# Layer 0's seams reordered, and some attention biases in another pool, in a two-layer FNet/Hyena/attention backbone

## The chip, the cores and the metric

The kernel runs on one core of a Trainium2 chip. The core has a matrix engine (TensorE, PE in the profile), VectorE (DVE), ScalarE (ACT) and GpSimd (POOL). SyncE (SP) has no arithmetic here: its queue issues DMA transfers, strictly in order, and so does GpSimd's queue beside its own work. PEld is TensorE's loading of the stationary operand. On-chip memory is SBUF, and matmuls accumulate in PSUM.

The metric is the device time of one execution in microseconds (us). A profiled execution also gives a span, from the first to the last instruction. The granted clock is the share of its full clock at which TensorE was allowed to run in a stretch.

## The reference

The model has two layers over 1024 latent tokens (a 16 x 64 grid, width 1024) with 256 context tokens, in float32. Each layer is a mixer and a SwiGLU feed-forward part (FFN) of hidden width 2816, and each of the two is preceded by an RMS norm and modulated by six vectors (shift, scale and gate, twice) that come from a conditioning vector:

```python
def ada_mod(cond, w, b):
    m = (jax.nn.silu(cond) @ w + b)[..., None, :]
    return jnp.split(m, 6, axis=-1)

def swiglu(u, w_gate, w_up, w_down):
    return (jax.nn.silu(u @ w_gate) * (u @ w_up)) @ w_down

def mixer_ab(u, w_in, w_out, conv_w, conv_b, w1, b1, freq, w2, b2, w3, skip):
    p = u @ w_in
    y_f = fourier_mix(p[..., :FOURIER_CH])
    y_h = hyena_mix(p[..., FOURIER_CH:], conv_w, conv_b, w1, b1, freq, w2, b2, w3, skip)
    return jnp.concatenate([y_f, y_h], axis=-1) @ w_out
```

Latent tokens are conditioned by `c`, context tokens by `c_ctx`. Layer 0's mixer is `mixer_ab`: four groups of channels through a two-dimensional Fourier transform, the others through a Hyena operator with two long convolutions. Layer 1's mixer is neighbourhood attention of 16 heads, in which a latent query sees an 8 x 32 window of the grid, with a relative position bias and a mask of columns, and all context keys. Layer 1 gives no context output. A final RMS norm ends the model.

## The kernel before

Activations stand with the channels on the 128 partitions, as eight blocks, and with the tokens on the free axis, in pieces `pc`: 0 and 1 are the two halves of the latent tokens (512 each), 2 is the context (256). Matrix products are made of three matmuls: every operand is split into a high part (a cast to fp32r, on ScalarE, line 350) and a low part (source less high, on VectorE, line 352), and TensorE sums high x high, high x low and low x high (`lin`, and `mm` in line 346). So a weight goes through four steps: its load by SP into a stage tile `ws` (a pool of four) or a wide tile `s` (pool `S4`), the cast to `wh`, the subtraction to `wl`, and 24 matmuls for one block of 128 outputs. In a block of the context, 256 tokens wide, the first two of every three matmuls use `wh` alone, so TensorE begins when `wh` is there and stands at the third if `wl` is not.

The order on each engine is made by a scheduler from the program's generators. `follow(x)` holds what is issued under it behind instruction `x` in the order; a `yield` in a generator is a place at which other work may be put. A tile of a pool is reused in turn, and the instruction that first writes it waits for the last reader of its previous use. SP works in order: a load that waits for its tile holds all loads behind it.

The four places that matter here follow each other in time.

`out_proj` (from about 640 us) is layer 0's output projection. While it runs, `late_groups` computes a group of modulation vectors on VectorE: `load_cond` loads `c` and `c_ctx`, broadcast to all partitions, in four pieces, and applies SiLU to each on ScalarE (line 556); products and row sums are line 584. Just before it, the last Hyena inverse transform ends with splits of its result `y` (`inverse_last`). An eviction (line 1739) adds a projected block to the residual `h`; `square` (lines 609 and 614) sums its squares over the blocks into a tile `tk`.

The first FFN (from 751 us) begins with the context: for each of 22 blocks `fb`, 24 matmuls of `gate` and 24 of `up`, SiLU of the gate (line 2011) and its product with up (line 2012). `rms_begin` turns the sums of squares into row sums with eight narrow matmuls, a square root and a reciprocal, and `rms_end` broadcasts the result over the partitions. From block 2 on, `wino_second` prepares, block by block, the second half of the latent operands for a Strassen-Winograd product that follows (lines 1809 to 1842).

`down` is the FFN's last product. Its latent part ends near 1494 us; then comes the context part, 22 blocks `kb` of 24 matmuls (line 2230), while `after2` norms the finished latent pieces for layer 1, block by block: two instructions on VectorE (lines 656 and 659) and one on ScalarE (658) for each.

The attention (until about 2080 us) goes through 64 items. An item loads a bias for two column groups of a head; items of the column groups 0 and 1 (`c0 == 0`) take two tiles of pool `G` for it, the others one `ws` tile. Line 2443 takes the maximum of the context scores, 2446 joins local scores and bias and reduces, 2448 and 2450 are the exponentials. In items before the 48th (`cross`) the exponentials of the context are transposed by DMA, from a tile of pool `TK`; in the last sixteen TensorE transposes them. In these last items SP also loads the attention's output back (`load_o`, `s<-d`) for the output projection.

Of the kernel before, what the change touches and what calls it, by code (L numbers as in the profile page):

```python
# [10 lines left out]
F32 = mybir.dt.float32  # L11
F32R = mybir.dt.float32r
F16 = mybir.dt.float16
AF = mybir.ActivationFunctionType
# [244 lines left out]
class Builder:  # L259
# [333 lines left out]

    def late_groups(self, ms, where):

        self.load_cond(wide=where == "s4")
        for m in ms:
            yield from self.ada_group(0, m, (0, 1), where)

# [815 lines left out]
    def inverse_last(self, y, fl):  # L1415

        nc, a = self.nc, self.a
        V = nc.vector
        C, x, late = [], [], []

        def product(acc, first, cb, m, e, i, f):
            yh, yl = (q[:, cb * P:cb * P + P] for q in self.y_of(1, i, f))
            d = acc[cb][:, e * 256:e * 256 + 256]
            for k, (s, w) in enumerate(((yh, m[:, :256]), (yh, m[:, 256:]), (yl, m[:, :256]))):
                nc.tensor.matmul(d, s, w, start=cb not in first, stop=e == 1 and i == 1 and f == 3 and k == 2,
                                 skip_group_check=True)
                first.add(cb)

        next(fl)
        for r in (0, 1):  # L1430
            acc = [self.PS() for _ in range(4)]
            first = set()
            ms = self.cmat2(a["vke_l"][r], True)
            for e, m in enumerate(ms):
                for cb in range(4):
                    for f in (0, 1):
                        product(acc, first, cb, m[:, f * 512:f * 512 + 512], e, 2 * e, 2 * r + f)
            yield
            if r == 0:
                next(fl)  # L1440
            else:
                for _ in fl:
                    yield
            ms = [self.cmat2(a["vko_l"][r, :, c:c + 2048], True) for c in (0, 2048)]
            if r:
                for cb in range(4):
                    x.append(self.S4())
                    self.ld(x[cb], self.xd[1][cb][:, :LAT])
            sa = [self.TK(), self.TK()]
            sa = [t[:, i:i + 256] for t in sa for i in (0, 256)]  # L1450
            for cb in range(4):
                for e, i in ((0, 3), (1, 1)):
                    for h, m in enumerate(ms[e]):
                        for f in (0, 1):
                            product(acc, first, cb, m[:, f * 512:f * 512 + 512], e, i, 2 * h + f)
                    if e == 0:
                        nc.scalar.copy(sa[cb], acc[cb][:, :256])
                A, B = sa[cb], acc[cb][:, 256:]
                t = self.G() if r == 0 else self.T()
                V.tensor_tensor(t[:, :256], A, B, ADD)  # L1460
                rv = t[:, 256:][:, ::-1]
                if r == 0:
                    V.tensor_tensor(rv, A, B, SUB)
                    C.append(t)
                    continue
                V.tensor_tensor(rv, B, A, SUB)
                y.t.update(self.new_act(pcs=(0, 1), wide=False, blocks=(4 + cb,)).t)
                v = self.T()
                V.tensor_tensor(v, C[cb], t, ADD)
                V.tensor_tensor(C[cb], C[cb], t, SUB)  # L1470
                V.tensor_tensor(v, v, x[cb][:, :512], MUL)
                self.split(v, y.ap(0, 4 + cb, 0), y.ap(1, 4 + cb, 0))
            yield
        for cb in range(4):
            V.tensor_tensor(C[cb], C[cb], x[cb][:, 512:], MUL)
            self.split(C[cb], y.ap(0, 4 + cb, 1), y.ap(1, 4 + cb, 1))

    def inverse_c(self, o, y):
        nc, a = self.nc, self.a
# [494 lines left out]
        s.to(2)  # L1974
        return s

    def ffn(self, l, u, h, hs, second, after, keep=None, begun={}):

        nc, a = self.nc, self.a
        n2 = NFB // 2  # L1980
# [19 lines left out]
        if l == 0:  # L2000
            self.pad(self.pt, PAD_T)
        if u is not None:
            for fb in range(NFB):
                wide = 3 if fb < NFB - 2 else 2
                gh, gl = self.weights(a["gate"][l, fb], wide=wide)
                uh, ul = self.weights(a["up"][l, fb], wide=wide)
                lo = self.last_lo
                ga = self.lin(gh, gl, 0, range(KB), u, (2,))[2]
                ua = self.lin(uh, ul, 0, range(KB), u, (2,))[2]
                t = self.T()  # L2010
                nc.scalar.activation(t[:, :256], ga[:, :256], AF.Silu)
                nc.vector.tensor_tensor(t[:, :256], ua[:, :256], t[:, :256], MUL)
                self.ldr(hidc[fb // 2][:, fb % 2], t[:, :256])
                if fb >= 2:
                    with self.follow(last):
                        next(second, None)
                last = lo
            self.load_cond(act=False)
            todo = (x for l1, m in [(0, 5)] + [(1, m) for m in range(6)]
                    for x in self.ada_group(l1, m, (0, 1) if l1 == 0 or m < 2 else (0,), "s4"))  # L2020
# [16 lines left out]
        for i in range(NFB // 2):  # L2037
# [26 lines left out]
            gate = dict(self.res)  # L2064
            for k in ((0, 0), (1, 1), (0, 1)):
                nc.scalar.activation(gate[k], gate[k], AF.Silu)
            t = self.G()
# [345 lines left out]
    def attn_item(self, head, hd, hf, c0, qs, kk, kc, vt, osb, out, cross):  # L2413

        nc, a = self.nc, self.a
# [3 lines left out]
        if c0:  # L2419
            t = self.W("ws", "bias", F32, 768)  # L2420
            self.ld(t.rearrange("p (i k) -> p i k", i=2), a["bias"][head, hf, c0:c0 + 2].rearrange("i p k -> p i k"))
            bias = [t[:, :384], t[:, 384:]]
        else:
            bias = [self.G(F32, 384), self.G(F32, 384)]
            for i in (0, 1):
                self.ld(bias[i], a["bias"][head, hf, c0 + i])
        for i in (0, 1):
            c = c0 + i
# [3 lines left out]
        for i in (0, 1):  # L2432
            c = c0 + i
# [10 lines left out]
        pc = self.T()  # L2444
        for i in (0, 1):
# [3 lines left out]
                                 bias=mn[:, i:i + 1])  # L2449
# [10 lines left out]
        for k, src, n in turns:  # L2460
# [3 lines left out]
            t = self.S2(F16, 1024)  # L2464
# [6 lines left out]
        if not osb:  # L2471
            t = self.S4()
            osb.update({0: t[:, :512], 1: t[:, 512:]})
        for i in (0, 1):
            c = c0 + i
# [14 lines left out]
        for i in (0, 1):  # L2490
            c = c0 + i
# [39 lines left out]
    def run(self):  # L2531
        nc, a = self.nc, self.a
# [9 lines left out]
        def drain(g):  # L2542
            for _ in g:
                pass

        u = Act()
# [90 lines left out]
        h = Act()  # L2637
        u = None

        def load_h(pcs):  # L2640
            for pc in pcs:
                for b, t in enumerate(self.load_x(pc)):
                    h.put(0, b, pc, t)

        uf = Act()
        hs0 = [self.DR([P, 1280]) for _ in range(KB)]
        hs1 = [self.DR([P, 1280]) for _ in range(KB)]

        def spill(h, hs, pcs):
            for pc in pcs:  # L2650
                for b in range(KB):
                    self.ldr(hs[b][:, pc * 512:pc * 512 + WID[pc]], h.ap(0, b, pc))

        rest = []

        def after1(pcs):
            spill(h, hs0, pcs)
            if 2 in pcs:
                uf.t.update(self.new_act(pcs=(2,)).t)
                rs = self.rms(pcs)  # L2660
                for b in range(KB):
                    self.norm_block({b: h.ap(0, b, 2)}, b, 2, 0, 3, uf, rs[0])
                load_h((1,))
                rest.append(rs[1])
            else:
                drain(first)
                rest.append(self.rms((1,))[0])

        def first_row():
            yield from self.wino_first(h, 0, 3, rest.pop())  # L2670

        first = first_row()

        load_h((2, 0))
        self.out_proj("w_out", y, [(2, 0), (1,)], h, 0, 2, after1, first, late)
        for b in range(8):
            self.tap(f"h1_{b}", h.ap(0, b, 0))
        u1 = Act()
        hd = [self.DR([P, LAT]) for _ in range(KB)]

        def after2(pc):
            c = self.rms_begin(pc)
            yield
            r = self.rms_end(pc, c)
            yield
            for b in range(KB):
                if b % 2 == 0:
                    u1.t.update(self.new_act(pcs=(pc,), blocks=(b, b + 1)).t)
                self.norm_block({b: h3.ap(0, b, pc)}, b, pc, 1, 0, u1, r)
                if b % 2:  # L2690
                    yield

        h3 = Act()
        self.ffn(0, uf, h3, hs0, (x for r in rest for x in self.wino_second(h, 0, 3, r)), after2, hd)
        for b in range(8):
            self.tap(f"h2_{b}", h.ap(0, b, 0))
        for i, _ in enumerate(self.values(u1)):
# [62 lines left out]
        for i, _ in enumerate(first_part(1)):  # L2760
            if i == 7:
                c = self.rms_begin(0)
# [53 lines left out]
        begun = {(0, 0): self.wino_begin(1, 0, 0, self.G)}  # L2816
        c = self.rms_begin(1)
# [87 lines left out]
```

## Time and profile before

| | us |
|---|---|
| time, median of 3 runs (2848.43 to 2850.37) | 2848.94 |
| the profiled execution | 2850.4 |
| its span | 2848.5 |
| TensorE busy | 2762.6 (97%) |
| VectorE busy | 2044.6 (72%) |
| ScalarE busy | 1319.0 (46%) |
| GpSimd busy | 543.9 (19%) |

In rows of a timeline the first column is the start from the span's beginning, the second the duration of the group, then engine, line, operation, output and inputs by name, their shape, and the count; brackets hold the idle time of the engine just before and the instruction that ended it. A row of a busy engine says nothing of what the time depends on; an idle time of TensorE does, since it works 97% of the span.

### The profile page before, as it was taken

Reading aid. Unit: us, or ns where it says so; the run is one execution under the profiler, and the core shown is the slowest. Engines: PE = TensorE matmul, PEld = TensorE weight load, DVE = VectorE, ACT = ScalarE, POOL = GpSimd, SP = SyncE. Lnnn points to the kernel's source line nnn. Section 1 sums busy time; section 2 is a strip of 40 time slices with the busy share of each in tenths; the row PEclk is TensorE's granted clock in tenths of the full one; section 3 lists DMA queues with packets and bytes.
Section 4 is the critical chain, followed back from the end, with each engine's and each line's share of the span. In section 5 each row is a group of like instructions: output and inputs, shape, how many; then the busy total and the mean of one; then the engine's idle time right before and its main releaser. Section 6 shows DMA issues by size and latency. Waiting matters only on the chain. (4 is left out here: it accounts for less than half of the span.)

```text
span 2848.5 us, 43624 instructions
## 1 busy us (share of the span) xinstructions
PE 2762.6 (97%) x15610; PEld 2314.2 (81%) x15610; DVE 2044.6 (72%) x3531; ACT 1319.0 (46%) x2269; POOL 543.9 (19%) x880
## 2 busy tenths in 40 slices
PE   7999999999999999999999999999999999999998
PEld 4876778788898888888879888888887788888887
DVE  6767577867877888876777437778768977664556
ACT  5433336443554333333455337788755533333434
POOL 2210235331001221222020002333211122112000
PEclk9999999999999999999999999999999999999999
DMA  7356535665666656658884436877855366434763
GB/s 268 121 182 219 155 93 186 215 211 189 214 196 200 211 196 210 213 202 323 306 305 152 133 115 152 201 197 197 243 191 207 133 239 229 140 106 170 234 195 133
DMA packets 296886, 554.20 MB, mean 195 GB/s; under 512 B 81872, under 2 KB 128658, under 8 KB 296670
## 3 DMA queue, kind: packets, MB, share of 16 engines
q1 hardware_dynamic: 227966, 352.67, 39.4%
q0 software_dynamic: 61504, 185.65, 18.6%
q10 hardware_dynamic: 7200, 13.11, 1.4%
q8 instruction: 123, 2.02, 0.3%
q14 instruction: 93, 0.76, 0.1%
HBM read 405.01 MB, written 118.76 MB: 184 GB/s over the span
## 5 line engine op out<-in xcount | busy, mean ns | idle before, releaser
L1932 PE MATMUL ps<-s,s 128*128 128x512 f32 x2012 | 497.6, 391 | 3.5 <-DVE s L1823 1.9
L1932 PEld LDWEIGHTS ps<-s,s 128*128 128x128 f32 x2012 | 378.3, 188 | 84.0 <-DVE s L1823 3.2
L346 PE MATMUL ps<-s,wh 128*128 128x256 f32 (+1 forms) x1776 | 401.9, 331 | 10.8 <-ACT s L1043 3.2
L346 PEld LDWEIGHTS ps<-s,wh 128*128 128x128 f32 x1776 | 295.2, 190 | 46.4 <-ACT s L350 4.1
L346 PE MATMUL ps<-s,wl 128*128 128x256 f32 (+1 forms) x888 | 267.4, 329 | 1.7 <-DVE wl L352 1.6
L2109 PE MATMUL ps<-s,s 128*128 128x512 f32 (+1 forms) x1000 | 259.9, 383 | 3.3 <-DVE s L352 3.2
L350 ACT CAST s<-s 128x1024 fp32r<-128x1024 f32 (+2 forms) x192 | 172.6, 927 | 193.1 <-DMA s<-d 177.3
L346 PE MATMUL pq<-s,wh 128*128 128x512 f32 (+1 forms) x848 | 260.8, 389 | 0.4 <-ACT wh L350 0.3
L352 DVE TENSOR_TENSOR wl<-ws,wh 128x1024 fp32r<-128x1024 f32 (+1 forms) x141 | 168.3, 1195 | 119.8 <-ACT wh L350 114.2
L350 ACT CAST wh<-ws 128x1024 fp32r<-128x1024 f32 (+1 forms) x141 | 144.7, 1026 | 204.9 <-PE ps L346 85.0
L352 DVE TENSOR_TENSOR s<-s,s 128x1024 fp32r<-128x1024 f32 (+2 forms) x170 | 190.9, 1154 | 59.4 <-ACT s L350 59.1
L346 PE MATMUL ps<-s,s 128*128 128x65 f16 (+4 forms) x2736 | 226.2, 235 | 7.3 <-DVE st L2446 2.6
L350 ACT CAST s<-t 128x512 fp32r<-128x512 f32 (+2 forms) x238 | 133.9, 581 | 195.8 <-PE ps L1932 69.2
L2109 PEld LDWEIGHTS ps<-s,s 128*128 128x128 f32 x1000 | 184.5, 188 | 41.3 <-DVE s L352 5.0
L352 DVE TENSOR_TENSOR s<-t,s 128x512 fp32r<-128x512 f32 (+2 forms) x238 | 151.2, 651 | 72.6 <-ACT s L350 59.6
L1932 PE MATMUL ps<-s,wh 128*128 128x512 f32 x624 | 194.9, 390 | 0.0
L346 PEld LDWEIGHTS ps<-s,wl 128*128 128x128 f32 x888 | 165.6, 190 | 18.4 <-DVE wl L352 2.5
L337 POOL DMA_DIRECT2D d<-s x186 | 101.0, 544 | 375.5 <-DVE s L1739 92.5
L346 PEld LDWEIGHTS pq<-s,wh 128*128 128x128 f32 x848 | 151.1, 190 | 22.1 <-ACT wh L350 0.7
L346 PE MATMUL pq<-s,wl 128*128 128x512 f32 (+1 forms) x424 | 162.0, 382 | 0.6 <-DVE wl L352 0.6
L2109 PE MATMUL ps<-s 128*128 128x512 f32 (+1 forms) x500 | 150.9, 385 | 0.0
L346 PEld LDWEIGHTS ps<-s,s 128*128 128x128 f32 (+1 forms) x816 | 126.6, 192 | 21.8 <-ACT t L2448 2.7
(486 smaller groups left out, 5465.0 us busy)
## 6 DMA issues: line engine op xcount, KB each, us to landing
s<-d SPq DMA_DIRECT2D x282, 256.0 KB, 3.9
d<-s POOLq DMA_DIRECT2D x170, 256.0 KB, 3.7
s<-in_down SPq DMA_DIRECT2D x150, 256.0 KB, 4.2
s<-in_ada_w POOLq DMA_DIRECT2D x64, 512.0 KB, 4.9
ws<-in_up SPq DMA_DIRECT2D x44, 512.0 KB, 3.7
d<-g POOLq DMA_DIRECT2D x86, 256.0 KB, 3.0
ws<-in_gate SPq DMA_DIRECT2D x42, 512.0 KB, 4.8
d<-tk POOLq DMA_DIRECT2D x66, 256.0 KB, 4.0
```

Of the source, the lines that this page charges most:

```text
L337: self.last_ldr = self.nc.gpsimd.dma_start(out, in_).ins
L346: self.last_mm = self.nc.tensor.matmul(o, l, r, start=st, stop=sp).ins
L350: self.last_hi = nc.scalar.copy(hi, src).ins
L352: self.last_lo = eng.tensor_tensor(lo, src, hi.bitcast(F32), SUB).ins
L1932: nc.tensor.matmul(ps, x[:, sl], y, start=first and j == 0 and x is wh and y is xh, stop=j == 3 and x is wl, skip_group_check=True)
L2109: m = nc.tensor.matmul(acc[j][:, c0:c1], x[:, sl], y[:, xs], start=first and k == 0, stop=last and k == 2, skip_group_check=True)
```

## The change

1. `late_groups` loads the conditions without their SiLU, yields three times more, and then applies the four SiLUs behind the last cast of the inverse transform (`inv_hi`).
2. The row-sum matmuls of the second latent half are no longer made at the end of `out_proj` but as the first step of the work that goes along with the FFN's blocks: `rms_begin` behind block 0, `rms_end` behind block 1, and `wino_second` from block 2 on as before. The gate weight of block 0 is loaded and split earlier, during `wino_first`, and `p3 = 1` sets which tiles it takes.
3. `after2` norms the second latent half one block at a time, each behind the low split of a weight.
4. In attention items with `c0 == 0` that are neither `cross` nor of a pair's second head (`hd`), the two biases take tiles of pool `TK` in place of pool `G`.

```diff
     def late_groups(self, ms, where):
 
-        self.load_cond(wide=where == "s4")
+        self.load_cond(wide=where == "s4", act=False)
+        yield
+        yield
+        yield
+        with self.follow(self.inv_hi):
+            for t in self.cond:
+                for x in t:
+                    self.nc.scalar.activation(x, x, AF.Silu)
...
         for cb in range(4):
             V.tensor_tensor(C[cb], C[cb], x[cb][:, 512:], MUL)
             self.split(C[cb], y.ap(0, 4 + cb, 1), y.ap(1, 4 + cb, 1))
+        self.inv_hi = self.last_hi
...
         if u is not None:
+            last = None
             for fb in range(NFB):
                 wide = 3 if fb < NFB - 2 else 2
-                gh, gl = self.weights(a["gate"][l, fb], wide=wide)
+                gh, gl = early.pop() if fb == 0 else self.weights(a["gate"][l, fb], wide=wide)
...
-                if fb >= 2:
-                    with self.follow(last):
-                        next(second, None)
+                with self.follow(last):
+                    next(second, None)
                 last = lo
...
-            bias = [self.G(F32, 384), self.G(F32, 384)]
+            new = self.G if cross or hd else self.TK
+            bias = [new(F32, 384), new(F32, 384)]
...
                 drain(first)
-                rest.append(self.rms((1,))[0])
 
         def first_row():
-            yield from self.wino_first(h, 0, 3, rest.pop())
+            for k, _ in enumerate(self.wino_first(h, 0, 3, rest.pop())):
+                if k == 6:
+                    self.p3 = 1
+                    early.append(self.weights(a["gate"][0, 0], wide=3))
+                yield
...
+            los = []
             for b in range(KB):
                 if b % 2 == 0:
                     u1.t.update(self.new_act(pcs=(pc,), blocks=(b, b + 1)).t)
-                self.norm_block({b: h3.ap(0, b, pc)}, b, pc, 1, 0, u1, r)
-                if b % 2:
+                with self.follow(los.pop() if los and pc == 1 else None):
+                    self.norm_block({b: h3.ap(0, b, pc)}, b, pc, 1, 0, u1, r)
+                los.append(self.last_lo)
+                if b % 2 or pc == 1:
                     yield
...
+        def second():
+            with self.follow(self.last_mm):
+                c = self.rms_begin(1)
+            yield
+            with self.follow(self.last_mm):
+                r = self.rms_end(1, c)
+            yield
+            yield from self.wino_second(h, 0, 3, r)
```

What this does to the order is seen best at three places. In the rows a tile's name ends in a running number, which tells one use of a tile from another; lines after the first edit carry numbers that are some 7 to 9 higher than before.

VectorE at the FFN's blocks 2 and 3, before (`wl_7626` is the low part of gate 3's weight, `t_7547` the product of block 1):

```order
L352 TENSOR_TENSOR wl_7559<-s_2061_7557,wh_7558 128x1024
L1835 SCALAR_TENSOR_TENSOR s_1699_6932<-s_1699_6932,c_97,t_7269 128x512
L1823 TENSOR_TENSOR s_2069_7621<-s_1711_6980,s_2069_7621 128x512
L1842 TENSOR_TENSOR s_1725_7060<-s_1699_6932,s_1725_7060 128x512
L352 TENSOR_TENSOR wl_7626<-s_2070_7624,wh_7625 128x1024
L1823 TENSOR_TENSOR s_2079_7692<-s_1725_7060,s_2079_7692 128x512
L2012 TENSOR_TENSOR t_7547<-ps_7522,t_7547 128x256
```

and now (`t_7613` is the product of block 2, from up 2's result `ps_7588`):

```order
L352 TENSOR_TENSOR wl_7559<-s_2061_7557,wh_7558 128x1024
L2021 TENSOR_TENSOR t_7539<-ps_7514,t_7539 128x256
L1843 SCALAR_TENSOR_TENSOR s_1698_6930<-s_1698_6930,c_97,t_7543 128x512
L1843 SCALAR_TENSOR_TENSOR s_1699_6932<-s_1699_6932,c_97,t_7543 128x512
L1850 TENSOR_TENSOR s_1711_6980<-s_1698_6930,s_1711_6980 128x512
L1850 TENSOR_TENSOR s_1725_7060<-s_1699_6932,s_1725_7060 128x512
L1831 TENSOR_TENSOR s_2069_7621<-s_1711_6980,s_2069_7621 128x512
L1831 TENSOR_TENSOR s_2079_7692<-s_1725_7060,s_2079_7692 128x512
L2021 TENSOR_TENSOR t_7613<-ps_7588,t_7613 128x256
L352 TENSOR_TENSOR wl_7626<-s_2070_7624,wh_7625 128x1024
```

The first steps of `wino_second` and the product of block 2 now stand ahead of gate 3's low split.

VectorE in the context part of `down`, before (`t` and `s` belong to the norm, `wl` to the weights):

```order
L352 TENSOR_TENSOR wl_14519<-ws_14517,wh_14518 128x1024
L656 SCALAR_TENSOR_TENSOR t_14583<-s_3020_12687,c_99,t_14505 128x512
L656 SCALAR_TENSOR_TENSOR t_14587<-s_3021_12689,c_99,t_14505 128x512
L656 SCALAR_TENSOR_TENSOR t_14630<-s_3022_12691,c_99,t_14505 128x512
L656 SCALAR_TENSOR_TENSOR t_14634<-s_3023_12693,c_99,t_14505 128x512
L656 SCALAR_TENSOR_TENSOR t_14674<-s_3078_12968,c_99,t_14505 128x512
L659 SCALAR_TENSOR_TENSOR s_3328_14581<-t_14583,c_99,s_3328_14581 128x512
L352 TENSOR_TENSOR wl_14553<-ws_14551,wh_14552 128x1024
```

and now:

```order
L352 TENSOR_TENSOR wl_14519<-ws_14517,wh_14518 128x1024
L663 SCALAR_TENSOR_TENSOR t_14583<-s_3020_12687,c_99,t_14505 128x512
L666 SCALAR_TENSOR_TENSOR s_3328_14581<-t_14583,c_99,s_3328_14581 128x512
L352 TENSOR_TENSOR wl_14553<-ws_14551,wh_14552 128x1024
L663 SCALAR_TENSOR_TENSOR t_14624<-s_3021_12689,c_99,t_14505 128x512
L352 TENSOR_TENSOR wl_14596<-ws_14594,wh_14595 128x1024
L663 SCALAR_TENSOR_TENSOR t_14664<-s_3022_12691,c_99,t_14505 128x512
L666 SCALAR_TENSOR_TENSOR s_3329_14582<-t_14624,c_99,s_3329_14582 128x512
L666 SCALAR_TENSOR_TENSOR s_3341_14662<-t_14664,c_99,s_3341_14662 128x512
L352 TENSOR_TENSOR wl_14634<-s_3338_14632,wh_14633 128x1024
```

The norm's instructions now stand one to three between two splits.

SP in the last attention items, before (`s<-d` are the loads of the attention's output):

```order
L331 DMA s_4641_22126<-d_15887 128x512
L331 DMA g_22037<-in_bias 128x384
L331 DMA s_4642_22128<-d_15888 128x512
L331 DMA g_22038<-in_bias 128x384
L331 DMA bias_22343<-in_bias 128x2x384
```

and now:

```order
L331 DMA tk_21637<-in_bias 128x384
L331 DMA bias_21736<-in_bias 128x2x384
L331 DMA tk_22037<-in_bias 128x384
L331 DMA t_21520<-d_15137 32x4x128 x4
L331 DMA tk_22038<-in_bias 128x384
L331 DMA bias_21948<-in_bias 128x2x384
L331 DMA bias_22131<-in_bias 128x2x384
L331 DMA s_4584_21804<-d_15877 128x512
```

The two biases of this item moved from the end of the stream of `s<-d` loads to a place ahead of its first one.

More of the change, by code (lines that the diff above doesn't have):

```diff
@@ L1975, in wino_begin, with ffn @@
         return s
-    def ffn(self, l, u, h, hs, second, after, keep=None, begun={}):
+    def ffn(self, l, u, h, hs, second, after, keep=None, begun={}, early=()):
         nc, a = self.nc, self.a
@@ L2652, in spill @@
                     self.ldr(hs[b][:, pc * 512:pc * 512 + WID[pc]], h.ap(0, b, pc))
-        rest = []
+        rest, early = [], []
         def after1(pcs):
@@ L2688, in after2 @@
                     u1.t.update(self.new_act(pcs=(pc,), blocks=(b, b + 1)).t)
-                self.norm_block({b: h3.ap(0, b, pc)}, b, pc, 1, 0, u1, r)
-                if b % 2:
+                with self.follow(los.pop() if los and pc == 1 else None):
+                    self.norm_block({b: h3.ap(0, b, pc)}, b, pc, 1, 0, u1, r)
+                los.append(self.last_lo)
+                if b % 2 or pc == 1:
                     yield
         h3 = Act()
-        self.ffn(0, uf, h3, hs0, (x for r in rest for x in self.wino_second(h, 0, 3, r)), after2, hd)
+        def second():
[6 more added lines that the diff above has]
+            yield from self.wino_second(h, 0, 3, r)
+        self.ffn(0, uf, h3, hs0, second(), after2, hd, early=early)
         for b in range(8):
```

## The prediction, made before the changed kernel was run

> **What bounds the kernel now.** I read the shares of busy time first, then the waits of TensorE from 500 us on, then the narrow stretches around the largest of them.
>
> ```profile
> PE 2762.6 (97%) x15610; PEld 2314.2 (81%) x15610; DVE 2044.6 (72%) x3531; ACT 1319.0 (46%) x2269; POOL 543.9 (19%) x880
> ```
>
> TensorE works 97% of a span of 2848.5 us: 85.9 us are idle in all, and an edit that leaves the matmuls alone can win only what lies in that, or in slow matmuls. So each of the four places of the change is read by one question: does TensorE stand still there, and who ends the standstill? The rows of the waits name a line, the releaser, the sum in us, how often, and the longest:
>
> ```profile
> PE ps L2230 <- DVE wl L352: 3.0, 2, 2.1
> PE ps L346 <- DVE st L2446: 2.6, 1, 2.6
> ...
> PE pq L346 <- DVE tk L614: 2.3, 1, 2.3
> ...
> PE ps L346 <- DVE wl L352: 1.6, 1, 1.6
> ```
>
> These four rows are the four places: `down`'s context part (two waits, 0.91 and 2.10), the attention's last items (2.57), the first FFN's start (2.29), and `out_proj` (1.63). A wait costs more than itself where the granted clock falls behind it. The columns of the next view are: stretch, its length, PE busy, PEld, DVE, ACT, POOL busy, the granted clock, DMA share, GB/s.
>
> ```profile
> 756.20:759.60 3.40, 3.40 (x19) 3.40 (x18) 2.23 (x4) 2.31 (x6) 0.00 (x0) 0.50 0.89 276
> ...
> 1537.90:1541.30 3.40, 3.40 (x16) 3.40 (x17) 3.40 (x5) 0.72 (x1) 0.00 (x0) 0.50 0.57 194
> ...
> 2060.10:2063.50 3.40, 3.40 (x14) 3.01 (x14) 2.15 (x7) 1.53 (x4) 0.30 (x1) 0.50 1.04 318
> ...
> 2070.30:2073.70 3.40, 3.32 (x35) 3.03 (x35) 1.88 (x7) 3.12 (x8) 0.00 (x0) 0.51 0.32 126
> ```
>
> Right behind the waits of 2.29, 2.10 and 2.57 us (and behind a pair of 0.94 and 0.97 at 2058 to 2060) TensorE runs 3.4 us at half clock, which loses 3.4 x 0.5 = 1.7 us each time. Behind the 1.63 in `out_proj` it does not:
>
> ```profile
> 670.80:674.20 3.40, 3.17 (x19) 2.83 (x20) 3.40 (x10) 0.00 (x0) 0.54 (x1) 1.00 0.60 184
> ```
>
> So I count a wait of about 2 us or more as itself plus 1.7, a shorter one as itself. The Trainium skill, "TensorE: Matmul & The Clock Gate", section "HAM oscillation — how this bites in real kernels", sets the limit higher: no idle gap of TensorE over about 3.4 us. The half clock in these rows follows standstills of 2.1 to 2.6 us, so the rows decide; what the time would be if the rule held is a rival below.
>
> **A: SiLUs of the conditions, `out_proj` (1.63 and a small 0.17 us).** The rows below are ScalarE's, then VectorE's.
>
> ```profile
> 654.18 0.63 ACT L556 ACTIVATE s<-s 128x512 f32<-128x512 f32 x1 [0.71 <-DMA s<-in_c_ctx]
> 654.72 1.64 ACT L350 CAST s<-g 128x512 fp32r<-128x512 f32 x3
> ```
> ```profile
> 653.50 0.69 DVE L352 TENSOR_TENSOR s<-t,s 128x512 fp32r<-128x512 f32 x1 [3.98 <-ACT s L350]
> ...
> 669.76 1.22 DVE L352 TENSOR_TENSOR wl<-ws,wh 128x1024 fp32r<-128x1024 f32 x1
> ```
>
> Four SiLUs wait one by one for the broadcast loads of c and c_ctx; casts of y's last splits stand behind them in ScalarE's order, and VectorE idles 3.98 us for them. It then works without a pause until the weight split at 669.76, which TensorE waits for. With the casts ahead of the SiLUs, five of those splits (one of 0.69, four more of the same form) fall into that idle time, so some 2 to 3 us leave the backlog, which is more than the 1.63 wait. The SiLUs themselves are bound by their loads (the last lands at about 654.2), and ScalarE's casts before them need no DMA, so the adaLN products are not later. Gain 1.63 + 0.17 = **1.8**; bounds 0 (the backlog stays, since adaLN products change places too) and 1.8.
>
> **B: the first FFN's start (2.29 us, then half clock).**
>
> ```profile
> 751.33 0.39 PE L346 MATMUL ps<-s,wl 128*128 128x512 f32 x1
> 754.01 1.05 PE L346 MATMUL pq<-c,tk 128*128 128x1 f32 x8 [2.29 <-DVE tk L614]
> ```
> ```profile
> 754.19 2.36 DVE L352 TENSOR_TENSOR wl<-s,wh 128x1024 fp32r<-128x1024 f32 x2 [0.24 <-ACT wh L350]
> ...
> 769.54 0.42 DVE L2012 TENSOR_TENSOR t<-ps,t 128x256 f32<-128x256 f32 x1
> 769.99 1.23 DVE L352 TENSOR_TENSOR wl<-s,wh 128x1024 fp32r<-128x1024 f32 x1
> ```
> ```profile
> 776.00:781.44 5.44, 5.44 (x50) 5.44 (x49) 4.75 (x7) 2.89 (x4) 0.54 (x1) 1.00 0.53 170
> ```
>
> The eight row-sum matmuls wait for the last eviction's square. The change puts them behind the second projection (up) of block 0 and has gate 0's weight split some 10 us earlier, so gate 0 starts at once: 2.29 + 1.7 = 3.99 go. Two waits come in. First, up 0's low half is split after the same eviction, as the first of the two at 754.19, and ends near 755.4. A projection of 24 matmuls takes 5.44 / 2 = 2.72 us (the row of 776.00 is one block), so gate 0 would end at 751.72 + 2.72 = 754.44, and up 0's third matmul, 0.22 later, waits 0.7. Second, the order of VectorE now has the gate-times-up product of block 2 *ahead of* the low split of gate 3, where before it stood behind it. That product needs up 2's last matmul, so gate 3's third matmul comes only a product and a split after that: 0.42 + 1.23 less the 0.22 of its first two matmuls, 1.4 us. Behind it gate 4's split stands ahead of the product again. Gain 3.99 - 0.7 - 1.4 = **1.9**. Bounds: 3.3 if gate 3 doesn't stall, 0.2 if that stall grows towards 2 us and brings a half clock (-1.7). Two more table loads on ScalarE fall in blocks where it works 2.89 of 5.44 us (row above); without that cover they would cost what they last.
>
> **C: `down`'s context part (0.91 and 2.10 us, then half clock).**
>
> ```profile
> 1527.45 3.40 DVE L656 SCALAR_TENSOR_TENSOR t<-s,c,t 128x512 f32<-128x512 f32 x5
> ...
> 1531.42 1.22 DVE L352 TENSOR_TENSOR wl<-ws,wh 128x1024 fp32r<-128x1024 f32 x1
> ...
> 1536.54 1.22 DVE L352 TENSOR_TENSOR wl<-ws,wh 128x1024 fp32r<-128x1024 f32 x1
> ```
> ```profile
> s<-in_down SPq DMA_DIRECT2D x150, 256.0 KB, 4.2
> ```
>
> Five norm instructions (3.40 us) run in one piece ahead of a split that TensorE needs at 1531.8, and seven more ahead of the next. After the change one to three stand between two splits. A block of weights lasts 24 matmuls, 2.72 us; a split and two norm instructions of 3.40 / 5 = 0.68 are 1.22 + 1.36 = 2.58, so VectorE just keeps pace. Removed: 3.01 + 1.7 = 4.71. What comes in is on the queue of SP: the wide tile that holds every fifth weight now gets its load behind that of a narrow one, which waits until a split has freed a tile.
>
> ```profile
> 1532.67 5.48 SPq L331 DMA_DIRECT2D ws<-in_down  x2
> ```
>
> Before, such a load went out at 1532.67, right after the split that began at 1531.42; with only two norm instructions ahead of that split it comes about 1 us earlier, and the wide load with it, near 1531.7. With 4.2 us to land (the row is of 256 KB; I take it for these of 512 KB too), the cast of 1.0 and the split of 1.22 that weight is ready near 1538.1, against a need at 1536.9: 1.2 us, and by the same walk 0.3 at the next of them. Gain 4.71 - 1.5 = **3.2**; bounds 4.7 (loads in time) and 0.5 (the first of them misses by 2.2, with a half clock).
>
> **D: biases of four of the last sixteen items (2.57 us, then half clock).**
>
> ```profile
> 2059.35 0.33 SPq L331 DMA_DIRECT2D g<-in_bias  x1
> ```
> ```profile
> 2069.70 0.62 DVE L2446 CUSTOM_DVE_ANT_0 g<-ps,g,st 128x384 f32<-128x384 f32 x1 [3.21 <-DMA g<-in_bias]
> ```
>
> The bias of such an item waits for a G tile, is issued at 2059.35 in the middle of the stream that loads the attention's output, and lands 10 us later behind it; the reduce holds the score's PSUM, and TensorE stops. In the other pool its load stands ahead of that stream. That pool has four tiles and, in these items, no other user, since the transposes of the first part are done; I find none of its four loads waiting for a tile, and what stands behind them (loads of t, the stream) comes earlier, not later. Gain 2.57 + 1.7 = **4.3**. Above it: ScalarE's wait at 2054.31
>
> ```profile
> 2054.31 0.84 ACT L350 CAST wh<-ws 128x768 fp32r<-128x768 f32 x1 [1.61 <-DMA ws<-in_w_out]
> ```
>
> is behind the pair of 0.94 and 0.97 with its half clock. If the stream, some 3.5 us earlier, makes room for that load, 0.94 + 0.97 + 1.7 = 3.6 go as well: upper bound 7.9. I take none of it, since the DMA engines stay full (share 1.04 in the row of 2060.10). Lower bound 0, a rival below.
>
> **Sum.** 1.8 + 1.9 + 3.2 + 4.3 = 11.2. The profiled execution took 2850.4, 1.9 outside its span, and is the slowest of three; from the median 2848.9 the sum gives **2838**. Its own range: all losses, 0 + 0.2 + 0.5 + 4.3 = 5.0, gives 2844; all gains, 1.8 + 3.3 + 4.7 + 7.9 = 17.7, gives 2831.
>
> **The rivals.**
>
> *Each seam gets its stall back* (0.17). B's gate 3 and C's first wide tile both stall 2 us or more, with a half clock each: 1.8 + 0.2 + 0.5 + 4.3 = 6.8, **2842**. For it: the half clock needs only about 0.5 us more than I give these two waits. Also, untouched waits of 1.6 to 1.8 us elsewhere may come to lie otherwise and get one, 1.7 each: 2844. Against it: the walks give 1.4 and 1.2.
>
> *All goes, the pair at 2058 too* (0.15): **2831**, as above.
>
> *The half clock doesn't come from these waits* (0.06). Then it stays, somewhere, and only bare waits go: 1.80 + 2.29 + 3.01 + 2.57 - 0.7 - 1.4 - 1.5 = 6.1, **2843**. Against it: each of the rows with 0.50 starts at or soon after the end of such a wait. The rule of the Trainium skill named above would make it so.
>
> *D doesn't do what it says* (0.06): a load of the new tiles waits for its tile on SP and holds the stream. Gain 1.8 + 1.9 + 3.2 = 6.9, **2842**.
>
> *Slower* (0.06): VectorE becomes the bound of the FFN's first part. It works 4.75 of 5.44 us in a block already. If the product stayed ahead of the next gate's low split in all following blocks, each would cost the 1.4 us of gate 3; against the gains of the rest, 1.8 + 3.2 + 4.3 + 3.99 - 0.7 = 12.6, nine blocks break even, and nineteen cost 26.6: 2849 + 14 = **2863**. Against it: the order has the split ahead again at gate 4, and 0.69 us a block are free to catch up.
>
> **How the numbers follow.** Forecast 0.50, rivals as given. What can be told from no change is 0.2% or 5.7 us, so faster means below 2843.2: nearly all of the forecast (0.48), all of the second rival (0.15), and a good half of those at 2842 to 2843 (0.14) make 0.77; slower 0.06; within it 0.17. The range 2830 to 2846 takes in all cases but the slower one and half clocks at several untouched waits.
>
> **What would show it.** Right: no wait of TensorE on wl in `out_proj`; gate 0 directly behind `out_proj`'s last matmul, a wait of 0.7 at up 0 and of 1.4 at gate 3; full clock at about 754 to 758, 1534 to 1540 and 2062 to 2072; norm instructions singly between splits; the biases landed before 2040. Wrong: a new wait of 2 us or more at gate 3 or at a wide tile, SP standing before a bias of the new pool, or half clocks that remain where no wait precedes them.

## The result, and the profile after

| | us |
|---|---|
| changed kernel, median of 11 runs (2837.0 to 2849.5) | 2843.3 |
| before, 11 runs (2848.4 to 2861.4) | 2850.4 |
| ratio, 95% interval | 0.997 (0.9957 to 0.9983) |
| the changed kernel a second time, 6 runs against 11 of before, ratio | 0.9966 (0.9953 to 0.9978) |
| profiled executions: before, after | 2850.4, 2839.6 |

The change makes the kernel 0.30% to 0.34% faster, 8.6 to 9.7 us of 2850; the first interval allows 4.8 to 12.3 us. The forecast was 11.2 us less, 2838, with a range of 2830 to 2846. The two profiled executions differ by 10.8 us, close to the forecast, but that agreement is luck in part: what the four places give differs from the forecast in each, and the differences cancel. These are the rows per core, first before, then after:

```profile
core 0: 2848.5 us, clock 0.990
```
```profile
core 0: 2837.8 us, clock 0.993
```

In every clock record of this case's traces TensorE's clock is either full or half. The records give 58 us at half clock before and 37 us after. Of that difference of 21 us, 13.7 lie between 640 and 2100 us, where the four places are: four stretches before, none after. The rest lies where nothing was changed.

What each place gives can be read without the rest of the program: from the start of one matmul to the start of another that both kernels have. Each of these stretches holds the same number of matmuls in both (lines of the kernel before):

| stretch | matmuls | before, us | after, us | less | forecast |
|---|---|---|---|---|---|
| A: first matmul of `out_proj` (line 1765) to the broadcast of the first latent half's norm | 456 | 85.96 | 84.50 | 1.5 | 1.8 |
| B: from there to the first matmul of the Winograd product (line 1932) | 1202 | 157.26 | 156.20 | 1.1 | 1.9 |
| C: first matmul of `down` (line 2109) to the first of line 2463 | 2220 | 446.67 | 444.83 | 1.8 | 3.2 |
| D: from there to the last matmul of line 2502 | 3865 | 405.75 | 398.08 | 7.7 | 4.3 |

Together they are 12.0 us shorter, and the rest of the span is 1.4 us longer. So B and C gave less than forecast, and D more, with the pair of waits at 2058 in it, which the forecast left out.

TensorE's waits between 640 and 2100 us, after the change (line, releaser, sum, times, longest; 2238 was line 2230 before, 2117 was 2109, 2476 was 2467):

```profile
PE ps L2117 <- DVE s L352: 1.6, 1, 1.6
PE ps L2238 <- DVE wl L352: 1.5, 2, 0.8
PE ps L346 <- DVE wl L352: 1.5, 2, 0.8
PE ps L346 <- DVE s L2476: 1.1, 3, 0.6
PE ps L2238 <- ACT wh L350: 0.9, 2, 0.8
PE ps L346 <- ACT wh L350: 0.7, 1, 0.7
```

The four rows of the prediction's second fence, 9.5 us together, are gone. Rows 2, 3, 5 and 6, 4.6 us, are new: the waits that the seams got in exchange. The first row was there before. Seam by seam:

**A.** The last four splits of y and the weight split on VectorE, after:

```profile
649.88 2.49 DVE L352 TENSOR_TENSOR s<-g,s 128x512 fp32r<-128x512 f32 x4
...
665.48 1.23 DVE L352 TENSOR_TENSOR wl<-ws,wh 128x1024 fp32r<-128x1024 f32 x1
```

The splits are done by 652.4, as the SiLUs begin, and the weight split comes at 665.48 in place of 669.76. The waits of 1.63 and 0.17 us are gone, 1.8 us, as predicted.

**B.** TensorE at the FFN's start, then VectorE at gate 3:

```profile
753.85 0.39 PE L346 MATMUL ps<-s,wl 128*128 128x256 f32 x1 [0.70 <-DVE wl L352]
756.55 0.95 PE L346 MATMUL pq<-c,tk 128*128 128x1 f32 x8
...
770.35 0.50 PE L346 MATMUL ps<-s,wh 128*128 128x256 f32 x2 [0.72 <-ACT wh L350]
771.61 0.39 PE L346 MATMUL ps<-s,wl 128*128 128x256 f32 x1 [0.76 <-DVE wl L352]
```
```profile
770.00 0.42 DVE L2021 TENSOR_TENSOR t<-ps,t 128x256 f32<-128x256 f32 x1
770.33 2.36 DVE L352 TENSOR_TENSOR wl<-s,wh 128x1024 fp32r<-128x1024 f32 x2
```

Up 0 waits 0.70, as predicted. Gate 3 waits 0.72 for its cast and 0.76 for its low half, 1.48 against a predicted 1.4, and the product of block 2 stands right ahead of that split. A part of the cause was not seen: the cast is late too, since on ScalarE it stands behind the two casts of `wino_second`.

**C.** ScalarE's casts of the two wide tiles in `down`:

```profile
1533.34 1.05 ACT L350 CAST wh<-s 128x1024 fp32r<-128x1024 f32 x1 [0.80 <-DMA s<-in_down]
...
1549.02 1.04 ACT L350 CAST wh<-s 128x1024 fp32r<-128x1024 f32 x1 [1.40 <-DMA s<-in_down]
```

The waits of 0.91 and 2.10 are gone. Both wide tiles land late, as the walk on SP's queue said. TensorE waits 0.17 + 0.76 at the first and 0.75 + 0.76 at the second, 2.4 us against a predicted 1.5.

**D.** SP and VectorE in the last items:

```profile
2020.01 0.36 SPq L331 DMA_DIRECT2D tk<-in_bias  x1
```
```profile
2058.44 0.61 DVE L2455 CUSTOM_DVE_ANT_0 tk<-ps,tk,st 128x384 f32<-128x384 f32 x1
```

The bias that landed at 2069.7 is now issued by 2020 and its instruction waits for nothing. The wait of 2.57 is gone, and no stretch between 640 and 2100 us has the half clock. The pair of 0.94 and 0.97 is one wait of 0.64.

### The profile page after: what moved, and what is told of

Its sections match the earlier page's. It is cut to its first block, busy times and chain, and to the rows that moved or that the text cites. A ratio compares the mean times of both kernels' runs of the same rounds, so it can differ in the third digit from the quotient of the medians.

```text
span 2837.8 us, 43617 instructions
## 1 busy us (share of the span) xinstructions
PE 2755.4 (97%) x15610; PEld 2309.6 (81%) x15610; DVE 2043.9 (72%) x3531; ACT 1321.2 (47%) x2271; POOL 544.0 (19%) x880
```

## The experiments

### One part at a time

Each kernel is the one before with the hunks of one part of the diff. For B these are all that name `early`, `second` or `last`, for C those with `los`, for D the two lines with `new`.

> Part A alone (SiLUs behind the casts; nothing else changed). If the casts behind the SiLUs made the weight's low half late: the waits of TensorE of 1.63 and 0.17 us in out_proj are gone and the other three places keep theirs; 1.8 us less. If the backlog on VectorE came from the adaLN products themselves: a wait of 1 to 2 us stays somewhere in out_proj, and the time doesn't move.

> Part B alone (row sums behind block 0, gate 0's weight early). If the seam is worth what its waits show: the wait of 2.29 us is gone, waits of 0.7 us at up 0 and of 1.4 to 1.5 us in two pieces at gate 3 stand in its place, no half clock behind them; from the end of out_proj to the start of gate 3 about 2 us less. If the half clock behind the 2.29 us has another cause, it is still there and the stretch is only 0.1 us shorter.

> Part C alone (norm blocks singly between the context's weights in down). If VectorE's order was the cause: the waits of 0.91 and 2.10 us are gone, and about 0.9 and 1.5 us stand at the two wide tiles, without a half clock; 4.7 - 2.4 = 2.3 us less from 1500 to 1565 us. If the half clock is independent of the wait, only 0.6 us less.

> Part D alone (four items' biases in the other pool). If the bias loads behind the output's stream were the cause: the wait of 2.57 us and its half clock are gone, 4.3 us; and if the stream's earlier start also serves the weight load before it, the pair of 0.94 and 0.97 shrinks to about 0.6 us and loses its half clock, 7.2 us in all. If the pair in the changed kernel shrank because the earlier parts moved the clock's grid or the queue, it stays near 1.9 us here and the gain is 4.3 us.

| part | TensorE's waits at its place, before to alone | ratio, 95% interval |
|---|---|---|
| A | 1.80 to none | 0.9991 (0.9980 to 1.0002) |
| B | 2.29 to 0.70 + 1.32 | 1.0005 (0.9996 to 1.0014) |
| C | 0.91 + 2.10 to 1.05 + 1.21 | 0.9998 (0.9988 to 1.0009) |
| D | 2.57 to none | 0.9982 (0.9973 to 0.9991) |

In every trace the waits went as expected, so what causes them is shown. The times say that D carries the gain (2.6 to 7.7 us), A probably the rest (5.7 less to 0.6 more), and B and C next to nothing: their intervals, -1.1 to +4.0 and -3.4 to +2.6 us, leave out or barely touch the 1.9 and 3.2 predicted.

The stretches of the result's table say more, since they leave out what varies elsewhere. The last three kernels are described further below; a number in bold is of a kernel that has the part:

| kernel | A, us | B, us | C, us | D, us |
|---|---|---|---|---|
| before | 86.0 | 157.3 | 446.7 | 405.8 |
| A alone | **84.1** | 155.6 | 445.1 | 403.0 |
| B alone | 86.7 | **160.1** | 445.1 | 402.8 |
| C alone | 87.2 | 157.2 | **445.0** | 405.9 |
| D alone | 87.8 | 156.9 | 445.5 | **397.5** |
| the change | **84.5** | **156.2** | **444.8** | **398.1** |
| the change, second profile | **84.1** | **156.2** | **445.1** | **398.4** |
| A and D | **83.7** | 157.2 | 445.5 | **397.8** |
| biases by GpSimd's queue | 86.0 | 157.3 | 448.1 | 398.0 |
| the change, mended | **84.1** | **154.3** | **442.9** | **397.8** |

A takes 1.5 to 4.1 us off its stretch and D 4.5 to 8.5, more than the 4.3 predicted. C alone takes 1.7 us off against this profile of before, where 2.3 were expected, but 0.1 to 0.5 against the 445.1 to 445.5 of the four others that lack it and have neither half clock nor slower pace there (both are explained below). The whole change takes about 1 us off B's stretch as it is with a half clock behind the wait of 2.29; in A's own kernel none came, and the stretch takes 155.6. B alone makes it 2.9 us longer, where some 2 us less were expected.

Two things that come by chance explain the spread in part: a slower pace and the half clock. The slower pace is B's. These are 100 us of the first FFN's context blocks, first before, then in B's kernel (in the brackets behind PE busy, the number of matmuls):

```profile
777.57:877.57 100.00, 100.00 (x884) 100.00 (x884) 72.99 (x91) 51.71 (x73) 10.80 (x20) 1.00 0.67 211
```
```profile
783.39:883.39 100.00, 100.00 (x851) 100.00 (x850) 72.35 (x89) 50.43 (x70) 10.63 (x20) 1.00 0.63 208
```

At full clock and without a wait TensorE does 884 matmuls in the one and 851 in the other: one every 0.113 us or every 0.118. That makes some 3.9 us in 100, about the whole distance from 160.1 to the 156.2 of the changed kernel. Eight other traces hold 884 or 885 here. The C stretch of 448.1 has the slower pace too (0.118 us from 1545 to 1583). In the kernels with artificial waits below, the pace is the one or the other from one wait to the next (in the first of them 0.118 us from 825 to 832, 0.113 from 842 to 849). What sets it, and whether it holds in B's other executions, stays open.

The half clock shows at D's place. A's own kernel keeps D's wait, 3.40 us long in its profile, and B's keeps it with 3.41. TensorE in the one, then in the other:

```profile
2065.61 0.56 PE L346 MATMUL ps<-s,s 128*128 128x65 f16 x13 [3.40 <-DVE st L2454]
```
```profile
2071.71 0.47 PE L346 MATMUL ps<-s,s 128*128 128x65 f16 x10 [3.41 <-DVE st L2446]
```

And the stretches around them, again A's kernel first (the eighth column is the granted clock):

```profile
2060.60:2064.00 3.40, 1.61 (x13) 1.30 (x12) 0.30 (x1) 0.48 (x1) 0.55 (x1) 1.00 1.03 390
2064.00:2067.40 3.40, 1.79 (x34) 1.66 (x34) 1.76 (x7) 1.81 (x5) 0.00 (x0) 1.00 0.89 344
2067.40:2070.80 3.40, 3.40 (x24) 3.07 (x23) 3.40 (x10) 2.96 (x9) 0.00 (x0) 1.00 0.06 22
```
```profile
2069.20:2072.60 3.40, 0.89 (x30) 0.89 (x30) 0.90 (x3) 0.91 (x3) 0.22 (x1) 1.00 1.06 404
2072.60:2076.00 3.40, 3.40 (x17) 3.11 (x14) 2.33 (x7) 2.21 (x7) 0.00 (x0) 0.50 0.32 125
```

The clock changes only at multiples of 3.413 us from one another, in every trace to within 0.01 us; where that grid lies relative to the program differs from run to run. The windows above are periods of that grid. In A's kernel it cuts the wait of 3.40 into 1.79 and 1.61 of idle time, and no half clock follows. In B's kernel 2.51 of 3.41 lie in one period, and the next one is at 0.50. The prediction's rule, by the length of the wait, gave both the 1.7 us.

### Waits of known length

In the kernel before, blocks 4 to 20 of the first FFN, every second one, get an artificial wait:

```diff
-                ga = self.lin(gh, gl, 0, range(KB), u, (2,))[2]
+                probes = {4: 0, 6: 1, 8: 2, 10: 3, 12: 4, 14: 5, 16: 1, 18: 2, 20: 3}
+                with self.follow(self.last_mm if fb - 1 in probes else None):
+                    ga = self.lin(gh, gl, 0, range(KB), u, (2,))[2]
...
+                n = probes.get(fb)
+                if n is not None:
+                    src = t[:, 256:384] if n else t[:, :128]
+                    for k in range(n):
+                        nc.gpsimd.tensor_tensor(src, src if k else t[:, 128:256], t[:, :128], SUB)
+                    with self.follow(self.last_mm):
+                        self.mm(ua[:, 256:257], src, self.ones[:, 0:1], True, True)
```

> The kernel before, with a standstill of TensorE put behind every second block of the first FFN's context part, blocks 4 to 20: an extra matmul of one column that reads the block's product after 0, 1, 2, 3, 4, 5, 1, 2, 3 subtractions on GpSimd (its result is not used). Waits from about 0.7 us in steps of about 0.5 us. If a wait of about 2 us or more brings the half clock: none behind the waits under 1.6 us, a stretch of 3.4 us at 0.5 behind nearly all over 2.2 us, and mixed between, by where the wait lies in the clock's grid. If only gaps over 3.4 us bring it: at most one such stretch, behind the longest. If the half clock comes by time and not by waits: stretches that don't follow the waits' lengths.

> As probe1 with 2, 1, 3, 2, 1, 2, 3, 6, 1 subtractions at the same blocks, so that waits near 2 us meet the clock's grid of 3.41 us at other places. If what counts is the idle time within one period of that grid, of two waits of equal length the one that lies within a period brings the half clock and the one that is cut in the middle doesn't. If the length alone counts, equal waits do equally.

The steps were coarser than expected (waits of 0.55 and of 2.4 to 5.6 us), but the grid cut them at many places. The same wait of 2.79 us, in the first and in the second of these kernels:

```profile
802.57 0.38 PE L346 MATMUL ps<-c,t 128*128 128x1 f32 x2 [2.79 <-POOL t L2020]
```
```profile
808.62 0.38 PE L346 MATMUL ps<-c,t 128*128 128x1 f32 x2 [2.79 <-POOL t L2020]
```

and the periods of the clock around them, in the same order:

```profile
800.20:803.60 3.40, 1.03 (x8) 1.03 (x9) 2.81 (x4) 0.59 (x1) 1.92 (x2) 1.00 0.61 193
803.60:807.00 3.40, 3.40 (x18) 3.40 (x17) 0.95 (x2) 0.62 (x1) 0.00 (x0) 0.50 0.00 0
```
```profile
803.80:807.20 3.40, 2.03 (x18) 1.83 (x17) 2.80 (x5) 2.16 (x4) 0.55 (x2) 1.00 0.63 206
807.20:810.60 3.40, 1.98 (x17) 1.98 (x18) 2.67 (x3) 0.60 (x1) 1.37 (x1) 1.00 0.36 137
810.60:814.00 3.40, 3.40 (x32) 3.40 (x32) 1.85 (x2) 1.35 (x3) 0.00 (x0) 1.00 0.00 0
```

With 2.4 us of the wait in one period, the next is at half clock. Cut into 1.4 and 1.4, the same wait is followed by full clock. Over the 18 waits, of the periods that began at full clock, each with 1.99 us or more of idle time is followed by the half clock (eleven with 2.0 to 3.3, and two that are idle throughout); each with 1.72 or less is not; of those between, 1.74 was and 1.75 and 1.77 were not. In three of the 13 cases, where the wait reached into the period at half clock, that lasted for two periods. So behind these waits what counts is the idle time within one period of the grid, and the limit is near half a period. Elsewhere it is less sharp: over all traces, periods with 1.3 to 1.94 us of idle time are followed by either clock, and each with more by the half clock. At some places less is enough; at the FFN's start in the profile of before it was 1.28 us:

```profile
752.80:756.20 3.40, 2.12 (x16) 1.92 (x17) 2.70 (x3) 3.40 (x5) 0.54 (x1) 1.00 0.20 80
756.20:759.60 3.40, 3.40 (x19) 3.40 (x18) 2.23 (x4) 2.31 (x6) 0.00 (x0) 0.50 0.89 276
```

About 1 us of the 2.12 busy ones is the eight row-sum matmuls, one column wide each. So idle time is not the whole measure; what is measured beside it stays open.

### A and D without B and C, the change again, and the two stalls mended

> Parts A and D without B and C. If the four parts add up from their waits, with the half clock counted by the clock's grid (about half of the times for a wait of 2.1 to 2.6 us): A 1.8, D 2.6 to 4.7 plus about 1, in all 6 to 7 us less than before, and 2 to 3 us more than the whole change. If B and C are worth 5.1 us as predicted: 5 us more than the whole change.

> The changed kernel once more, beside A and D alone and beside the mended one on the same chip. If B and C are worth 2 to 3 us: 8 to 10 us less than before. In the trace: waits of 0.7 at up 0, 1.5 at gate 3 and 0.7 to 0.8 in two pieces at each wide tile, as in the first profile, and half clocks at other places than there, since the grid lies otherwise; none where the idle time within one period of the grid is under 1.8 us, in the stretches where the matmuls stand close.

The mended kernel differs from the changed one so:

```diff
                 ga = self.lin(gh, gl, 0, range(KB), u, (2,))[2]
+                if fb == 0:
+                    next(second)
...
                 with self.follow(last):
-                    next(second, None)
+                    if fb != 1:
+                        next(second, None)
...
+                for k in (kb, kb + 2) if kb == 0 else (kb + 2,):
+                    if k % 5 == 4 and k < NFB:
+                        wide[k] = self.S4()
+                        self.ld(wide[k].rearrange("p (r k) -> p r k", r=2), w[k].rearrange("r p k -> p r k"))
-                f = self.W("ws", "ws") if kb % 5 < 4 else self.S4()
+                f = self.W("ws", "ws") if kb % 5 < 4 else wide.pop(kb)
...
-                    self.ld(f.rearrange("p (r k) -> p r k", r=2), w[kb].rearrange("r p k -> p r k"))
+                    if kb % 5 < 4:
+                        self.ld(f.rearrange("p (r k) -> p r k", r=2), w[kb].rearrange("r p k -> p r k"))
```

> The whole change, with the two new stalls mended: the row sums go behind gate 0 (not up 0) and the broadcast behind up 0, so that the product of block 2 falls behind gate 3's low split again; and the wide tiles' loads in down's context part are issued two blocks ahead of their turn. If those stalls come from the order and from the loads' place on SP: the waits of 1.5 at gate 3 and of 1.5 and up to 1.5 at the wide tiles are gone and the time is 3 to 4.5 us less than the changed kernel's. If VectorE is the bound there: the stalls come back one block or one weight later, and the time is the changed kernel's.

| kernel | median us (range) | ratio, 95% interval |
|---|---|---|
| before | 2853.0 (2848.1 to 2856.5) | |
| A and D | 2842.8 (2840.2 to 2845.8) | 0.9966 (0.9954 to 0.9978) |
| the whole change | 2841.4 (2838.3 to 2849.5) | 0.9966 (0.9953 to 0.9978) |
| the whole, mended | 2837.6 (2836.4 to 2839.7) | 0.9949 (0.9937 to 0.9962) |

A and D alone give all of the change's gain that can be measured; against the 6 to 7 us expected they gave 6.3 to 13.1. The 2 to 3 us by which they should have stayed behind the whole change don't show: the medians differ by 1.4, and the ratios are equal. B and C, as written, hand back most of what they win. The waits of the mended kernel between 640 and 2100 us:

```profile
PE ps L2120 <- DVE s L352: 1.6, 1, 1.6
PE ps L2120 <- ACT s L350: 1.1, 1, 1.1
PE ps L346 <- DVE s L2485: 1.0, 2, 0.7
PE pq L346 <- ACT t L645: 0.7, 1, 0.7
PE ps L1773 <- DVE wl L352: 0.4, 1, 0.4
PE ps L1773 <- DVE t L1473: 0.2, 1, 0.2
```

Neither gate 3 nor a wide tile stalls. The 0.7 at up 0 is gone too, which was not expected; a new 0.7 stands where the broadcast waits for ScalarE, and 1.1 in `down`'s latent part, ahead of the new loads, whose cause stays open. Over the changed kernel the medians say 3.9 us, as expected. The two intervals against before overlap (10.8 to 18.0 us for the mended one), but the stretches show where it lies: 1.9 us at B and 1.9 to 2.1 at C, one profile of the mended kernel against two of the changed. In the change's second profile the waits at the four places are as in its first (0.71, 0.72 and 0.76 in the FFN, 0.20 + 0.76 at the first wide tile), but the second tile's cast is in time and only its 0.76 is left. A half clock lies at 2602 us, behind an untouched wait that was 2.01 us long; in the first profile that wait was 1.67 and brought none.

### What made the biases late

> The kernel before, with these biases (all items of column groups 0 and 1 whose bias is not cross or of a second head, the same four of the last sixteen) still in pool G, but loaded by GpSimd's queue in place of SP's. If what made them late was the place behind the output's stream on SP: they land earlier, and the wait of 2.6 to 4.7 us at 2070 shrinks below 1 us. If the tile of pool G comes free too late: the wait stays above 2 us, only GpSimd's queue stands instead of SP's.

```diff
             bias = [self.G(F32, 384), self.G(F32, 384)]
             for i in (0, 1):
-                self.ld(bias[i], a["bias"][head, hf, c0 + i])
+                (self.ld if cross or hd else self.ldr)(bias[i], a["bias"][head, hf, c0 + i])
```

GpSimd's queue, then VectorE:

```profile
2055.82 0.58 POOL L337 DMA_DIRECT2D g<-in_bias  x1 [4.56 <-PE ps L2463]
2056.58 0.56 POOL L337 DMA_DIRECT2D g<-in_bias  x1 [0.18 <-ACT s L2466]
```
```profile
2069.40 0.61 DVE L2446 CUSTOM_DVE_ANT_0 g<-ps,g,st 128x384 f32<-128x384 f32 x1
```

In this trace the attention starts 6.5 us later than before (first matmul of line 2463 at 1733.36 and 1726.82), so 2055.82 stands for some 2049 there: 10 us earlier than SP issued the load. It still goes out late compared with the changed kernel's (2020), behind 4.56 us of idle time that the tile's release ends. But it is in time: the instruction at 2069.40 waits for nothing and the wait of 2.57 is gone. D's stretch takes 398.0 us, as with the other pool. So it was the place in the stream on SP, not the pool's size alone. The other pool avoids both. The kernel was run once, for its profile.

## Why the prediction was right or wrong

- *The four waits and their causes*: right. Each part alone takes its own waits away and leaves those of the others.
- *A, 1.8*: right in its waits. Its stretch is 1.5 us shorter in the two profiles and 1.5 to 4.1 over all of them; the time alone, 2.6 less with 5.7 less to 0.6 more, agrees but doesn't show it by itself.
- *B's new waits, 0.7 and 1.4*: right in place and size (0.70 and 1.48); yet the stretch gained 1.1 us and not 1.9, and what took the rest stays open. *C's new waits, 1.5*: right in place, too small; measured 2.4 and 2.3, and 1.7 in the change's second profile. In the first two of these profiles it is the second wide tile that was underrated: 0.3 predicted, 1.2 to 1.5 measured.
- *D, 2.57 and what stands behind it*: right in cause, and the wait is longer in other executions (3.40, 3.41, 4.67 us in the three traces of single parts that keep it; 2.57 in the profile that was read). The prediction took one execution's value for the place's. The term was too small: D's stretch lost 7.7 us in the two profiles, 4.5 to 8.5 over all. That this made up for B and C, with 1.1 and 1.8 in place of 1.9 and 3.2, is luck.
- *"I count a wait of about 2 us or more as itself plus 1.7"*: this step failed. A half clock needs some 1.75 us of idle time within one period of a grid that lies anew in each run. A wait of g us at a random place then meets it in (3.41 + g - 2 x 1.75) / 3.41 of the cases: 0.59 for 2.10, 0.65 for 2.29, 0.73 for 2.57, an estimate. With 1.7 times that, the sum reads A 1.8, B 2.29 + 1.1 - 2.18 = 1.2, C 3.01 + 1.0 - 2.4 = 1.6, D 2.57 + 1.2 = 3.8: 8.4 us in place of 11.2, beside 8.6 and 9.7 measured; but for D it is no nearer to the stretches. The profile of before had the half clock behind each of the three long waits. Of the eight traces that keep B's wait of 2.29, seven have it; of the eight that keep C's 2.10, before alone; of the six that keep D's, five. So it is C's term that the one profile misled most, and the estimate looks too high for C and too low for the FFN's start.
- *The Trainium skill's limit of 3.4 us of idle time* (page "TensorE: Matmul & The Clock Gate", section "HAM oscillation — how this bites in real kernels"), the prediction's third rival: too high for this case. Waits of 2.1 to 2.8 us bring the half clock here; one of 3.40, at the limit itself, doesn't. That the window runs freely, as the Trainium skill says on the same page (section "Part 1: The HAM clock gate"), the traces confirm, with 3.413 us; it was this that the prediction left out of its sum.
- *The pair of 0.94 and 0.97, "go as well"*: open. It is 0.6 to 0.8 us in all five profiles with D, but B's kernel, which has not D, shows 0.7, C's 1.3 and A's 1.9. So it varies without D, and D is not shown to be its cause.
- *Range and chances*: the range held, though its lower end of the gains, 5.0 us, counts D with 4.3 where D's own lower bound is 0. The rival "each seam gets its stall back" is nearest to what happened to B and C, only without the half clocks that its price was made of.

## What to carry to other kernels

A wait of the busiest engine is worth its length plus a penalty that comes by chance; before counting the penalty, lay the clock's own grid over several profiles, or see in how many of them it comes. To learn what one place gives, compare the time between two matmuls that both kernels have, and not two spans. Moving a step off one wait moves the queue order of three engines: find the next instruction that now stands ahead of the split or load that the matmuls need (here a product, two casts, a narrow tile's load), since two of four seams gave back most of what they won there and a second small edit kept it. A load that is late behind a stream can be saved by the queue or by the tile; test which.

## What was not expected of the hardware

The clock's grid of 3.413 us runs freely, and its phase against the program differs in each run. Two waits of equal length, 2.79 us, cost 2.8 us and 2.8 + 1.7 us, by 1 us of difference in where they began on the grid.

At full clock, without a wait, the same matmuls of 256 columns run at one of two paces, 0.113 or 0.118 us apart. In one kernel the slower one cost 3.9 us over 100, more than three of the four places were expected to win.

Two profiles of one and the same kernel differ by 2.6 us: 2837.8 with a mean clock of 0.993 and 2840.4 with 0.992. That is as much as a whole seam, so the spans of two profiles could not have told B or C from nothing.
